# Row skewness of a 1024x8192 matrix: eight input buffers, finer transfers towards the end, and the closing arithmetic split between ScalarE and GpSimd

## The chip, the cores and the metric

The kernel runs on one core of one Trainium2 chip. The core has five engines that this document abbreviates as the profile does: PE (TensorE, matrix multiplies and transposes), DVE (VectorE), ACT (ScalarE), POOL (GpSimd) and SP (SyncE, which here only starts transfers). Sixteen DMA engines move data between the chip's memory and the on-chip buffers. The metric is device time in microseconds of one execution; lower is better.

## The reference

Each of the 1024 rows has 8192 float32 values. For each row the skewness is wanted:

```python
mean = np.mean(x, axis=-1, keepdims=True)
std = np.std(x, axis=-1, keepdims=True)
z = (x - mean) / (std + 1e-8)
return np.mean(z ** 3, axis=-1).astype(np.float32)
```

Both kernels reach it through the three raw moments of a row, m1, m2 and m3 (the means of x, x² and x³): the variance is m2 − m1², and the skewness is (m3 − 3·m1·m2 + 2·m1³) · variance^(−3/2). One pass over the 33.55 MB of input is enough.

## The kernel before

The rows are cut into eight blocks of 128, one row to a partition. A block's 8192 columns are cut into units, and a unit is one transfer, one buffer and one round of work. Block 0 has units of 512, 1024, 2560 and 4096 columns, blocks 1 to 6 have two units of 4096 each, and block 7 has 2048, 2048, 2048, 1024, 512 and 512 (lines 16 and 17): 22 units in all, u0 to u21. One loop runs over them in order.

For a unit, SP starts the transfer into an input buffer x (line 98); there are six such buffers (X_BUFS, line 18), so the transfer of unit u waits until everything that reads unit u−6 has ended. Three engines then work on the unit:

- ACT squares it into a buffer sq, one instruction per unit, and its accumulator gives the unit's share of m2 (line 101).
- DVE multiplies sq by x in one instruction per unit, and its accumulator gives the unit's share of m3 (line 105). It needs the square of the same unit, all of it, so it starts after ACT has ended the unit.
- PE transposes the unit in chunks of 128 columns, all into one PSUM tile tp, where they add up (line 117).

When a block's last unit is through, ACT copies tp to a tile tsb (line 127), PE multiplies tsb by a column of 1/8192, which gives the block's m1 (line 129), and ACT copies that column out of PSUM (line 130). ACT waits for PE between the two copies, for each of the eight blocks, and whatever follows on ACT waits behind.

After the loop, all eight blocks are closed together on tiles of 128x8: two sums over the units' shares (line 136), the products and the variance (lines 150, 151, 167 to 174), a square root on ACT (line 154), a reciprocal with a refining step (lines 156 to 164), the third power (lines 178 and 179) and the last product (line 181). A transpose on PE (line 184), a copy out of PSUM (line 187) and one transfer (line 188) end the program.

Each engine runs its own instructions in program order, and waits for other engines through semaphores that the framework places.

Of the kernel before, what the change touches and what calls it, by code (L numbers as in the profile page):

```python
# [1 line left out]

# [7 lines left out]
FP = mybir.dt.float32  # L10
AF = mybir.ActivationFunctionType
ALU = mybir.AluOpType
X_AXIS = mybir.AxisListType.X

W_MAIN = 4096
FIRST_UNITS = [512, 1024, 2560, 4096]
LAST_UNITS = [2048, 2048, 2048, 1024, 512, 512]
X_BUFS = 6
SQ_BUFS = 5


def _plan_units(NB, C):
    units = []
    for b in range(NB):
        if b == 0:
            ws = FIRST_UNITS
        elif b == NB - 1:
            ws = LAST_UNITS
        else:
            ws = [W_MAIN] * (C // W_MAIN)  # L30
        assert sum(ws) == C
        s = 0
        for w in ws:
            units.append((b, s, s + w))
            s += w
    return units


@with_exitstack
def kernel(  # L40
    ctx: ExitStack,
    tc: tile.TileContext,
    x: bass.AP,
    out: bass.AP,
):
    nc = tc.nc
    P = nc.NUM_PARTITIONS
    R, C = x.shape
    NB = R // P
    inv_n = 1.0 / float(C)  # L50
    import math as _m
    s_scale = float(1.0 / _m.sqrt(C))

    units = _plan_units(NB, C)
    NU = len(units)
    first_unit = {}
    unit_count = {}
    for u, (b, _, _) in enumerate(units):
        first_unit.setdefault(b, u)
        unit_count[b] = unit_count.get(b, 0) + 1  # L60
    MAXC = max(unit_count.values())
    NS = NB * MAXC

    def ucol(u):
        b = units[u][0]
        return b * MAXC + (u - first_unit[b])

    xv = x.rearrange("(b p) c -> b p c", p=P)
    ob = out.rearrange("(b p) -> b p", p=P)

    xpool = ctx.enter_context(tc.tile_pool(name="xp", bufs=X_BUFS))
    sqpool = ctx.enter_context(tc.tile_pool(name="sqp", bufs=SQ_BUFS))
    onep = ctx.enter_context(tc.tile_pool(name="onep", bufs=1))
    psum = ctx.enter_context(tc.tile_pool(name="ps", bufs=2, space=bass.MemoryType.PSUM))
    psum1 = ctx.enter_context(tc.tile_pool(name="ps1", bufs=1, space=bass.MemoryType.PSUM))

    ident = onep.tile([P, P], FP, tag="ident")
    make_identity(nc, ident)
    onesn = onep.tile([P, 1], FP, tag="onesn")
    nc.vector.memset(onesn, inv_n)  # L80

    s2u = onep.tile([P, NS], FP, tag="s2u")
    s3u = onep.tile([P, NS], FP, tag="s3u")
    s1pe = onep.tile([P, NB], FP, tag="s1pe")
    nc.vector.memset(s2u, 0.0)
    nc.vector.memset(s3u, 0.0)

    tiny = onep.tile([P, 8], FP, tag="tiny")
    nc.scalar.activation(out=tiny[:, 0:1], in_=onesn, func=AF.Sqrt)  # L89

    Tsb = [onep.tile([P, P], FP, tag=f"tsb{i}", name=f"tsb{i}") for i in range(2)]

    tp_psum = {}
    for u, (b, cs, ce) in enumerate(units):
        w = ce - cs
        uc = ucol(u)
        xt = xpool.tile([P, w], FP, tag="x", name=f"x_{u}")
        nc.sync.dma_start(out=xt, in_=xv[b, :, cs:ce])  # L98

        sq = sqpool.tile([P, w], FP, tag="sq", name=f"sq_{u}")  # L100
        nc.scalar.activation(  # L101
            out=sq, in_=xt, func=AF.Square, scale=s_scale,
            accum_out=s2u[:, uc : uc + 1],
        )
        nc.vector.scalar_tensor_tensor(  # L105
            out=sq, in0=sq, scalar=1.0, in1=xt, op0=ALU.mult, op1=ALU.mult,
            accum_out=s3u[:, uc : uc + 1],
        )

        if b not in tp_psum:  # L110
            tp_psum[b] = psum.tile([P, P], FP, tag="tp", name=f"tp_{b}")
        tpw = tp_psum[b]
        nchunk = w // P
        firstpe = (u == first_unit[b])
        lastpe = (u == first_unit[b] + unit_count[b] - 1)
        for c in range(nchunk):
            nc.tensor.matmul(  # L117
                out=tpw,
                lhsT=xt[:, c * P : (c + 1) * P],
                rhs=ident,  # L120
                start=(firstpe and c == 0),
                stop=(lastpe and c == nchunk - 1),
                is_transpose=True,
            )
        if lastpe:
            tsb = Tsb[b % 2]
            nc.scalar.copy(out=tsb, in_=tpw)  # L127
            s1ps = psum.tile([P, 1], FP, tag="s1ps", name=f"s1ps_{b}")
            nc.tensor.matmul(out=s1ps, lhsT=tsb, rhs=onesn, start=True, stop=True)  # L129
            nc.scalar.copy(out=s1pe[:, b : b + 1], in_=s1ps)  # L130

    fin = ctx.enter_context(tc.tile_pool(name="fin", bufs=1))

    def blocksum(name, src):
        dst = fin.tile([P, NB], FP, name=name)
        nc.vector.tensor_reduce(  # L136
            out=dst,
            in_=src.rearrange("p (b c) -> p b c", c=MAXC),
            axis=X_AXIS,
            op=ALU.add,  # L140
        )
        return dst

    m1 = s1pe
    m2 = blocksum("s2", s2u)
    m3 = blocksum("s3", s3u)

    m1sq = fin.tile([P, NB], FP)
    var = fin.tile([P, NB], FP)
    nc.vector.tensor_tensor(out=m1sq, in0=m1, in1=m1, op=ALU.mult)  # L150
    nc.vector.tensor_tensor(out=var, in0=m2, in1=m1sq, op=ALU.subtract)  # L151

    sig = fin.tile([P, NB], FP)
    nc.scalar.activation(out=sig, in_=var, func=AF.Sqrt)  # L154
    r0 = fin.tile([P, NB], FP)
    nc.vector.reciprocal(out=r0, in_=sig)  # L156
    t1 = fin.tile([P, NB], FP)
    nc.vector.tensor_tensor(out=t1, in0=r0, in1=r0, op=ALU.mult)  # L158
    nc.vector.tensor_tensor(out=t1, in0=t1, in1=var, op=ALU.mult)  # L159
# [3 lines left out]
    rr = fin.tile([P, NB], FP)  # L163
    nc.vector.tensor_tensor(out=rr, in0=r0, in1=t1, op=ALU.mult)  # L164

    aa = fin.tile([P, NB], FP)
    nc.vector.tensor_tensor(out=aa, in0=m1, in1=m2, op=ALU.mult)
    bb = fin.tile([P, NB], FP)
    nc.vector.tensor_tensor(out=bb, in0=m1sq, in1=m1, op=ALU.mult)
    num = fin.tile([P, NB], FP)  # L170
    nc.vector.scalar_tensor_tensor(
        out=num, in0=aa, scalar=-3.0, in1=m3, op0=ALU.mult, op1=ALU.add
    )
    nc.vector.scalar_tensor_tensor(
        out=num, in0=bb, scalar=2.0, in1=num, op0=ALU.mult, op1=ALU.add
    )
    r3 = fin.tile([P, NB], FP)
    nc.vector.tensor_tensor(out=r3, in0=rr, in1=rr, op=ALU.mult)  # L178
    nc.vector.tensor_tensor(out=r3, in0=r3, in1=rr, op=ALU.mult)  # L179
    skew = fin.tile([P, NB], FP)  # L180
    nc.vector.tensor_tensor(out=skew, in0=num, in1=r3, op=ALU.mult)  # L181

    skT_ps = psum1.tile([NB, P], FP, tag="skT")
    nc.tensor.matmul(out=skT_ps, lhsT=skew, rhs=ident, start=True, stop=True,  # L184
                     is_transpose=True)
    skT = fin.tile([NB, P], FP)
    nc.vector.tensor_copy(out=skT, in_=skT_ps)  # L187
    nc.sync.dma_start(out=ob, in_=skT)

# [29 lines left out]
```

## Time and profile before

| | |
|---|---|
| device time, median of 3 runs | 98.76 us (98.6 to 98.96) |
| span of the profiled execution | 97.4 us |
| median less span | 1.36 us |
| DVE busy | 73.8 us (76%) |
| PE busy | 67.3 us (69%) |
| ACT busy | 65.2 us (67%) |
| POOL busy | 0.7 us (1%), 6 instructions |
| bytes read | 33.55 MB, 344 GB/s over the span |

The span runs from the first to the last instruction of one profiled execution. The records give no device time of that one execution on its own, so the 1.36 us between its span and the median of the runs stand for what lies around it. A time "at 74.88" below is counted in microseconds from the span's start. A timeline row gives the start, the duration, the engine, the line, the operation with its tiles, and in brackets how long the engine had been idle and what released it. A row of the windows view gives a stretch of the span, its length, the busy time of PE, PE's weight loads, DVE, ACT and POOL in it (with the number of instructions), the granted TensorE clock, the busy share of the DMA engines, and the GB/s that they moved.

### The profile page before, as it was taken

To read this page: it belongs to the slowest core of one execution; us is meant where nothing else is said; L and a number is where in the kernel's file an instruction comes from. 1 tells how busy PE (TensorE), PEld (TensorE's weight loads), DVE (VectorE), ACT (ScalarE), POOL (GpSimd) and SP (SyncE) were. 2 spreads that over 40 slices of the span, in tenths; PEclk is the share of its full clock that TensorE was granted. 3 is DMA by queue.
4 is the path that set the end of the run, shared out by engine and by line. 5 is a ranking of instruction groups with operands and counts; after the bars stand their busy time and mean duration, and the time that the engine had idled before them with its cause. 6 is when DMAs were issued, how large, how long until landed. Compare 5 with 4: busy or idle time off the path is not lost.

```text
span 97.4 us, 1323 instructions
## 1 busy us (share of the span) xinstructions
PE 67.3 (69%) x529; PEld 62.2 (64%) x529; DVE 73.8 (76%) x64; ACT 65.2 (67%) x63; POOL 0.7 (1%) x6
## 2 busy tenths in 40 slices
PE   0480969695399999695969596959695998951010
PEld 0260959594398999594959495949594988940000
DVE  0250091498937929999999897989898979999961
ACT  6340909695293899795969597959695998990000
POOL 2000000000000000000000000000000000000000
PEclk9999999999958999999999999999999999999755
DMA  1999999999999999999999999999999993300000
GB/s 61 338 353 446 431 431 431 431 437 431 424 431 431 431 431 417 431 431 424 417 431 431 431 424 431 431 417 431 431 400 417 424 396 146 116 4 0 0 0 2
DMA packets 3190, 33.64 MB, mean 345 GB/s; under 512 B 360, under 2 KB 368, under 8 KB 1008
## 3 DMA queue, kind: packets, MB, share of 16 engines
q1 hardware_dynamic: 3184, 33.56, 82.5%
q8 instruction: 4, 0.07, 0.3%
q14 instruction: 2, 0.02, 0.1%
HBM read 33.55 MB, written 0.00 MB: 344 GB/s over the span
## 4 chain that ended last, share of the span: by engine, by line
DMA 62%; DVE 12%; issue 11%; ACT 7%; PE 4%; SPq 2%; DVEq 0%; ACTq 0%
DMA x<-in_x_dram 62%; DVE sq L105 9%; ACT sq L101 7%; PE tp L117 3%; SPq L98 2%; PE skT_ps L184 0%; DVE skT L187 0%; DVE s L136 0%; DVE t L160 0%; DVE rr L164 0%; DVE skew L181 0%; DVE t L158 0%; DVE r L179 0%; DVE r L178 0%; DVE t L159 0%
## 5 line engine op out<-in xcount | busy, mean ns | idle before, releaser
L105 DVE SCALAR_TENSOR_TENSOR sq<-sq,x 128x4096 f32<-128x4096 f32 (+4 forms) x22 | 71.1, 3260 | 19.9 <-ACT sq L101 19.7
L117 PE MATMUL tp<-ident,x 128*128 128x128 f32 x512 | 64.2, 287 | 17.1 <-DMA x<-in_x_dram 17.1
L117 PEld LDWEIGHTS tp<-ident,x 128*128 128x128 f32 x512 | 60.1, 148 | 19.9 <-DMA x<-in_x_dram 16.5
L101 ACT ACTIVATE sq<-x 128x4096 f32<-128x4096 f32 (+4 forms) x22 | 59.3, 2696 | 16.8 <-DMA x<-in_x_dram 16.8
L129 PEld LDWEIGHTS s1ps<-onesn,tsb 128*128 128x128 f32 x16 | 2.4, 188 | 5.9 <-ACT tsb L127 5.9
L129 PE MATMUL s1ps<-onesn,tsb 128*128 128x1 f32 x16 | 3.1, 260 | 4.0 <-ACT tsb L127 4.0
L184 PE MATMUL skT_ps<-ident,skew 128*8 128x128 f32 x1 | 0.4, 377 | 6.6 <-DVE skew L181 6.6
L184 PEld LDWEIGHTS skT_ps<-ident,skew 128*8 128x8 f32 x1 | 0.1, 84 | 6.7 <-DVE skew L181 6.7
L101 ACT ACTIVATION_READ_ACCUMULATOR sq<-x 128x1 f32 x22 | 4.1, 184 | 0.0
L130 ACT COPY s1pe<-s1ps 128x1 f32<-128x1 f32 x8 | 1.3, 159 | 3.8 <-PE s1ps L129 3.8
L127 ACT COPY tsb<-tp 128x128 f32<-128x128 f32 x8 | 2.1, 260 | 1.8 <-PE tp L117 1.7
L154 ACT ACTIVATE sig<-var 128x8 f32<-128x8 f32 x1 | 0.2, 208 | 4.5 <-DVE var L151 4.5
L105 DVE DVE_READ_ACCUMULATOR sq<-sq,x 128x1 f32 x22 | 1.8, 83 | 0.0
L89 ACT ACT_TABLE_LOAD x1 | 1.3, 1283 | 0.7 <-PEq L203 0.7
L80 DVE MEMSET onesn<- 128x1 f32 x1 | 0.1, 59 | 0.8 <-PEq L203 0.8
L187 DVE COPY skT<-skT_ps 8x128 f32<-8x128 f32 x1 | 0.3, 278 | 0.5 <-PE skT_ps L184 0.5
masks.py:199 POOL TENSOR_SCALAR_AFFINE_SELECT ident<-ident 128x128 f32<-128x128 f32 x1 | 0.3, 292 | 0.1
L89 ACT ACTIVATE tiny<-onesn 128x1 f32<-128x1 f32 x1 | 0.2, 203 | 0.0
masks.py:197 POOL MEMSET ident<- 128x128 f32 x1 | 0.2, 204 | 0.3 <-POOLq L203 0.3
L136 DVE TENSOR_REDUCE s<-s3u 128x8 f32<-128x48 f32 x1 | 0.2, 203 | 0.0
L156 DVE RECIPROCAL r<-sig 128x8 f32<-128x8 f32 x1 | 0.2, 203 | 0.0
L136 DVE TENSOR_REDUCE s<-s2u 128x8 f32<-128x48 f32 x1 | 0.2, 200 | 0.0
(19 smaller groups left out, 2.7 us busy)
## 6 DMA issues: line engine op xcount, KB each, us to landing
x<-in_x_dram SPq DMA_DIRECT2D x13, 2048.0 KB, 21.0
x<-in_x_dram SPq DMA_DIRECT2D x3, 1024.0 KB, 16.2
x<-in_x_dram SPq DMA_DIRECT2D x1, 1280.0 KB, 8.0
x<-in_x_dram SPq DMA_DIRECT2D x2, 512.0 KB, 6.9
x<-in_x_dram SPq DMA_DIRECT2D x3, 256.0 KB, 2.5
out_dram<-skT SPq DMA_DIRECT2D x1, 4.0 KB
```

The costliest lines, as they stand in the source:

```text
L89: nc.scalar.activation(out=tiny[:, 0:1], in_=onesn, func=AF.Sqrt)
L98: nc.sync.dma_start(out=xt, in_=xv[b, :, cs:ce])
L101: nc.scalar.activation(out=sq, in_=xt, func=AF.Square, scale=s_scale, accum_out=s2u[:, uc : uc + 1],)
L105: nc.vector.scalar_tensor_tensor(out=sq, in0=sq, scalar=1.0, in1=xt, op0=ALU.mult, op1=ALU.mult, accum_out=s3u[:, uc : uc + 1],)
L117: nc.tensor.matmul(out=tpw, lhsT=xt[:, c * P : (c + 1) * P], rhs=ident, start=(firstpe and c == 0), stop=(lastpe and c == nchunk - 1), is_ ...
L127: nc.scalar.copy(out=tsb, in_=tpw)
L129: nc.tensor.matmul(out=s1ps, lhsT=tsb, rhs=onesn, start=True, stop=True)
L130: nc.scalar.copy(out=s1pe[:, b : b + 1], in_=s1ps)
L136: nc.vector.tensor_reduce(out=dst, in_=src.rearrange("p (b c) -> p b c", c=MAXC), axis=X_AXIS, op=ALU.add,)
L154: nc.scalar.activation(out=sig, in_=var, func=AF.Sqrt)
L184: nc.tensor.matmul(out=skT_ps, lhsT=skew, rhs=ident, start=True, stop=True, is_transpose=True)
L187: nc.vector.tensor_copy(out=skT, in_=skT_ps)
```

## The change

The change alters five things.

1. **Units.** Blocks 0 to 2 keep their units. The later blocks are cut as in the diff, down to 256 columns for the last unit; there are 31 units instead of 22. There are eight input buffers instead of six.
2. **Slices.** A unit of more than 2304 columns is transferred whole, but ACT and DVE work on it in two slices. There are four sq buffers instead of five, each as large as the largest slice. In the last two units of block 7 ACT writes the square to PSUM, and DVE writes its product to a tile of its own.
3. **Block closing.** All eight m1 columns stay in one PSUM tile. The copy of line 130 is gone, and with it ACT's wait for PE after each block.
4. **Blocks 0 to 6** are closed when block 6 is through, ahead of block 7's work in the program: two sums on DVE, three small ACT instructions that read the m1 columns, and six GpSimd instructions on 128x7, one of them a power with the exponent −1.5.
5. **Block 7** is closed alone on 128x1 tiles: its m2 sum, variance and helpers on ACT, one power on GpSimd, and a sum and two products on DVE. The square root, the reciprocal and the refining step are gone. The rest of the program's end is as before.

```diff
-FIRST_UNITS = [512, 1024, 2560, 4096]
-LAST_UNITS = [2048, 2048, 2048, 1024, 512, 512]
-X_BUFS = 6
-SQ_BUFS = 5
+UNITS = [
+    [512, 1024, 2560, 4096],
+    [4096, 4096],
+    [4096, 4096],
+    [4352, 3840],
+    [3328, 2816, 2048],
+    [2048, 2048, 2048, 2048],
+    [1792, 1792, 1664, 1536, 1408],
+    [1152, 1152, 1152, 1152, 1024, 896, 896, 512, 256],
+]
+SUB_MAX = 2304
+X_BUFS = 8
+SQ_BUFS = 4
+PSUM_SQ = 2
+
+
+def _slices(w):
+    n = -(-w // SUB_MAX)
+    step = -(-w // n // 128) * 128
+    return [(s, min(s + step, w)) for s in range(0, w, step)]
...
+    def finish_first_blocks():
+
+        m2, m3 = small("m2a", L), small("m3a", L)
+        for dst, src in ((m2, s2u), (m3, s3u)):
+            nc.vector.tensor_reduce(
+                out=dst, in_=src.rearrange("p (b c) -> p b c", c=MAXC), axis=X_AXIS, op=ALU.add
             )
...
+        nc.scalar.activation(out=m1sq, in_=s1ps[:, 0:L], func=AF.Square)
+        nc.scalar.activation(out=m1sq3, in_=s1ps[:, 0:L], func=AF.Square, scale=third)
+        nc.scalar.activation(out=nm1, in_=s1ps[:, 0:L], func=AF.Copy, scale=-3.0)
+        g = nc.gpsimd
...
+        g.tensor_tensor(out=var, in0=m2, in1=m1sq, op=ALU.subtract)
+        g.tensor_tensor(out=m1sq3, in0=m1sq3, in1=var, op=ALU.add)
+        g.tensor_tensor(out=m1sq3, in0=m1sq3, in1=nm1, op=ALU.mult)
+        g.tensor_tensor(out=m3, in0=m3, in1=m1sq3, op=ALU.add)
+        g.tensor_tensor(out=rr, in0=var, in1=expo, op=ALU.pow)
+        g.tensor_tensor(out=skew[:, 0:L], in0=m3, in1=rr, op=ALU.mult)
+
+    def close_block(b, tp):
+        tsb = Tsb[b % 2]
+        nc.scalar.copy(out=tsb, in_=tp)
+        nc.tensor.matmul(out=s1ps[:, b : b + 1], lhsT=tsb, rhs=onesn, start=True, stop=True)
...
+            for s, e in _slices(w):
...
+                in_psum = last and k >= len(widths) - PSUM_SQ
+                pool = psq if in_psum else sqpool
+                sq = pool.tile([P, e - s], FP, tag="sq", name=f"sq_{b}_{k}_{s}")
+                nc.scalar.activation(
+                    out=sq, in_=xt[:, s:e], func=AF.Square, scale=s_scale, accum_out=a2
+                )
+                cube = cubes[:, 0 : e - s] if in_psum else sq
+                nc.vector.scalar_tensor_tensor(
+                    out=cube, in0=sq, scalar=1.0, in1=xt[:, s:e],
+                    op0=ALU.mult, op1=ALU.mult, accum_out=a3,
+                )
...
+        close_block(b, tp)
+        if b == L - 1:
+            finish_first_blocks()
...
+    nc.scalar.activation(out=junk, in_=s2l, func=AF.Copy, accum_out=m2)
+    nc.vector.tensor_reduce(out=m3, in_=s3l, axis=X_AXIS, op=ALU.add)
...
+    nc.scalar.activation(out=m1sq, in_=p1, func=AF.Square)
+    nc.scalar.activation(out=var, in_=m1sq, func=AF.Identity, scale=-1.0, bias=m2)
...
+    nc.gpsimd.tensor_tensor(out=rr, in0=var, in1=expo[:, 0:1], op=ALU.pow)
+    nc.scalar.activation(out=nm1, in_=p1, func=AF.Copy, scale=-3.0)
+    nc.scalar.activation(out=v3, in_=m1sq, func=AF.Identity, scale=1.0 / 3.0, bias=var)
     nc.vector.tensor_scalar(
-        out=t1, in0=t1, scalar1=-0.5, scalar2=1.5, op0=ALU.mult, op1=ALU.add
+        out=m3, in0=v3, scalar1=nm1, scalar2=m3, op0=ALU.mult, op1=ALU.add
     )
...
+    nc.vector.tensor_tensor(out=skew[:, L:NB], in0=m3, in1=rr, op=ALU.mult)
```

Here L is 7, the number of the last block, and s1ps is the PSUM tile with the eight m1 columns. The small ACT instruction at the program's start, which draws the activation table in, is a Square instead of a Sqrt.

More of the change, by code (lines that the diff above doesn't have):

```diff
@@ L49 @@
     NB = R // P
+    L = NB - 1
     inv_n = 1.0 / float(C)
[L51 to L66, printed above, removed]
+    s_scale = float(C) ** -0.5
+    third = (1.0 / 3.0) ** 0.5
+    assert len(UNITS) == NB and all(sum(u) == C for u in UNITS)
     xv = x.rearrange("(b p) c -> b p c", p=P)
     ob = out.rearrange("(b p) -> b p", p=P)
+    n_sub = [sum(len(_slices(w)) for w in u) for u in UNITS]
+    MAXC = max(n_sub[:L])
+    NL = n_sub[L]
     xpool = ctx.enter_context(tc.tile_pool(name="xp", bufs=X_BUFS))
@@ L74 @@
     psum = ctx.enter_context(tc.tile_pool(name="ps", bufs=2, space=bass.MemoryType.PSUM))
+    psq = ctx.enter_context(tc.tile_pool(name="psq", bufs=2, space=bass.MemoryType.PSUM))
     psum1 = ctx.enter_context(tc.tile_pool(name="ps1", bufs=1, space=bass.MemoryType.PSUM))
+    onesn = onep.tile([P, 1], FP, tag="onesn")
+    nc.vector.memset(onesn, inv_n)
+    tiny = onep.tile([P, 1], FP, tag="tiny")
+    nc.scalar.activation(out=tiny, in_=onesn, func=AF.Square)
     ident = onep.tile([P, P], FP, tag="ident")
@@ L78 @@
     make_identity(nc, ident)
[L79 to L84, printed above, removed]
+    s2u = onep.tile([P, L * MAXC], FP, tag="s2u")
+    s3u = onep.tile([P, L * MAXC], FP, tag="s3u")
     nc.vector.memset(s2u, 0.0)
     nc.vector.memset(s3u, 0.0)
-    tiny = onep.tile([P, 8], FP, tag="tiny")
-    nc.scalar.activation(out=tiny[:, 0:1], in_=onesn, func=AF.Sqrt)
@@ L91 @@
-    Tsb = [onep.tile([P, P], FP, tag=f"tsb{i}", name=f"tsb{i}") for i in range(2)]
[L93 to L123, printed above, removed]
-            )
[L125 to L150, printed above, removed]
@@ new lines, in close_block @@
+    def close_block(b, tp):
+        tsb = Tsb[b % 2]
+        nc.scalar.copy(out=tsb, in_=tp)
+        nc.tensor.matmul(out=s1ps[:, b : b + 1], lhsT=tsb, rhs=onesn, start=True, stop=True)
+    for b, widths in enumerate(UNITS):
+        last = b == L
+        tp = psum.tile([P, P], FP, tag="tp", name=f"tp_{b}")
+        c0 = 0
+        j = 0
+        for k, w in enumerate(widths):
+            xt = xpool.tile([P, w], FP, tag="x", name=f"x_{b}_{k}")
+            nc.sync.dma_start(out=xt, in_=xv[b, :, c0 : c0 + w])
+            c0 += w
+            for s, e in _slices(w):
+                i = b * MAXC + j
+                a2 = s2l[:, j : j + 1] if last else s2u[:, i : i + 1]
+                a3 = s3l[:, j : j + 1] if last else s3u[:, i : i + 1]
+                j += 1
+                in_psum = last and k >= len(widths) - PSUM_SQ
[9 more added lines that the diff above has]
+                )
+            n = w // P
+            for c in range(n):
+                nc.tensor.matmul(
+                    out=tp, lhsT=xt[:, c * P : (c + 1) * P], rhs=ident,
+                    start=(k == 0 and c == 0), stop=(c0 == C and c == n - 1),
+                    is_transpose=True,
+                )
+        close_block(b, tp)
+        if b == L - 1:
+            finish_first_blocks()
@@ L168 @@
[L168 to L179, printed above, removed]
@@ L180 @@
-    skew = fin.tile([P, NB], FP)
-    nc.vector.tensor_tensor(out=skew, in0=num, in1=r3, op=ALU.mult)
+    nc.vector.tensor_tensor(out=skew[:, L:NB], in0=m3, in1=rr, op=ALU.mult)
     skT_ps = psum1.tile([NB, P], FP, tag="skT")
-    nc.tensor.matmul(out=skT_ps, lhsT=skew, rhs=ident, start=True, stop=True,
-                     is_transpose=True)
-    skT = fin.tile([NB, P], FP)
+    nc.tensor.matmul(out=skT_ps, lhsT=skew, rhs=ident, start=True, stop=True, is_transpose=True)
+    skT = small("skT", P)[0:NB, :]
```

44 lines of the change are left out of this document (16 added, 28 removed).

## The prediction

> **What bounds the kernel now.** I read the page's slices first, then the chain, then the timeline of the end.
>
> ```profile
> DVE  0250091498937929999999897989898979999961
> DMA  1999999999999999999999999999999993300000
> GB/s 61 338 353 446 431 431 431 431 437 431 424 431 431 431 431 417 431 431 424 417 431 431 431 424 431 431 417 431 431 400 417 424 396 146 116 4 0 0 0 2
> DMA 62%; DVE 12%; issue 11%; ACT 7%; PE 4%; SPq 2%; DVEq 0%; ACTq 0%
> ```
>
> The transfers run at 431 GB/s up to about 80 us, then thin out, and from about 85 us on nothing arrives. The last twelve microseconds belong to DVE and to the closing arithmetic. So there are two stages: a stream, which the DMA engines set, and an end, which is the place to save. The timeline shows the end:
>
> ```profile
> 55.30 3.66 ACT L101 ACTIVATE sq<-x 128x4096 f32<-128x4096 f32 x1 [1.18 <-DMA x<-in_x_dram]
> 65.09 3.64 ACT L101 ACTIVATE sq<-x 128x4096 f32<-128x4096 f32 x1 [1.17 <-DMA x<-in_x_dram]
> 74.88 3.66 ACT L101 ACTIVATE sq<-x 128x4096 f32<-128x4096 f32 x1 [1.18 <-DMA x<-in_x_dram]
> 78.66 4.43 DVE L105 SCALAR_TENSOR_TENSOR sq<-sq,x 128x4096 f32<-128x4096 f32 x1 [0.50 <-ACT sq L101]
> 83.01 2.29 DVE L105 SCALAR_TENSOR_TENSOR sq<-sq,x 128x2048 f32<-128x2048 f32 x1
> 85.22 2.29 DVE L105 SCALAR_TENSOR_TENSOR sq<-sq,x 128x2048 f32<-128x2048 f32 x1
> 89.65 1.22 DVE L105 SCALAR_TENSOR_TENSOR sq<-sq,x 128x1024 f32<-128x1024 f32 x1
> 90.80 0.69 DVE L105 SCALAR_TENSOR_TENSOR sq<-sq,x 128x512 f32<-128x512 f32 x1
> 91.41 0.69 DVE L105 SCALAR_TENSOR_TENSOR sq<-sq,x 128x512 f32<-128x512 f32 x1
> 92.02 0.20 DVE L136 TENSOR_REDUCE s<-s2u 128x8 f32<-128x48 f32 x1
> 92.14 0.20 DVE L136 TENSOR_REDUCE s<-s3u 128x8 f32<-128x48 f32 x1
> ```
>
> Each ACT row was released by a landing, so these are landing times. The three rows are two units apart: 9.79 us for 8192 columns (4.19 MB), or 428 GB/s. Block 6's last unit, u15, lands at 74.88, ACT holds it to 78.6, and DVE takes it only from 78.66 to 83.01. Only then does DVE begin block 7, and it works without a gap until 92.02: 9.01 us for 8192 columns in six pieces. ACT has squared all of block 7 by then. The price of large units is thus the time from 74.88 to 83.01, in which a whole unit passes first through ACT and then through DVE.
>
> DVE's price by size, from one start to the next: 0.61 us for 512 columns (90.80 to 91.41), 1.15 for 1024, 2.21 for 2048, 4.35 for 4096. That is 1.045 ns a column and some 0.075 us a piece. A 4096 unit lands every 4.89 us, so DVE can keep up with the stream, and it can't catch up by much.
>
> **The transfers.**
>
> ```profile
> SPq L98 <- DVE sq L105: 73.8, 16, 7.4
> 78.23 5.26 SPq L98 DMA_DIRECT2D x<-in_x_dram  x2
> 4.90:7.00 2.10, 1.94 (x8) 1.54 (x8) 0.97 (x1) 1.10 (x2) 0.00 (x0) 1.00 0.96 341
> 78.00:79.00 1.00, 1.00 (x12) 1.00 (x10) 0.50 (x3) 1.00 (x3) 0.00 (x0) 1.00 1.02 414
> 80.00:81.00 1.00, 0.58 (x6) 0.34 (x5) 1.00 (x1) 0.67 (x3) 0.00 (x0) 1.00 0.79 305
> 81.00:82.00 1.00, 1.00 (x11) 1.00 (x12) 1.00 (x1) 0.86 (x2) 0.00 (x0) 1.00 0.40 150
> 82.00:83.00 1.00, 1.00 (x12) 1.00 (x11) 1.00 (x1) 1.00 (x1) 0.00 (x0) 1.00 0.12 47
> 83.00:84.00 1.00, 1.00 (x12) 1.00 (x10) 1.00 (x3) 1.00 (x3) 0.00 (x0) 1.00 0.04 16
> ```
>
> SP waits for DVE nearly always, but up to 79 us the engines stay full, so the wait costs nothing there, and two more buffers gain nothing in the stream. They matter at the end: u20 was started at 78.23 and u21 only about 83.2, when DVE had freed u15. With eight buffers the last transfer waits for block 7's first unit, which DVE leaves at about 80, some 5 us ahead of its turn. The windows from 80 to 84 also show that the sixteen engines don't end together: their mean share after 80 adds up to 0.79 + 0.40 + 0.12 + 0.04 = 1.35 us, yet two of them still work at 82 to 83 and one until about 83.6.
>
> More transfers cost something. At 78 to 79, with 1 MB units and full engines, 414 GB/s stand against 428: 1.05 MB takes 2.53 instead of 2.45 us, about 0.08 a transfer. Bounds: nothing, and 0.13 (half a megabyte at 305/0.79 = 386 GB/s against 428). I take 0.07. Up to the end of block 6 there are 22 transfers instead of 16, so its last unit lands at 74.88 + 6 x 0.07 = 75.3 (75.0 to 75.7), and all has landed at 75.3 + 9.79 + 7 x 0.07 = 85.6, counting nine transfers against two.
>
> The Trainium skill, "DMA: Bandwidth & Descriptors", section "Rules for kernel authors", speaks against this part: it asks for at least 1 MiB per transfer, and its measured table has 341 GB/s for one of 1 MB. Here 1 MB transfers run at 414 GB/s among others that are queued, so the trace disagrees for that size. By the page's rate the landings would be the bound, and the sum some 98.7 us (an estimate; rival C works out the same from a row of the trace).
>
> **From block 6 to block 7.** Units of 1792 down to 1408 columns land, by 1.195 ns a column, more slowly than DVE's 1.045 takes them, so no backlog has built up.
>
> ```profile
> 3.35 0.63 ACT L101 ACTIVATE sq<-x 128x512 f32<-128x512 f32 x1 [1.12 <-DMA x<-in_x_dram]
> 4.10 0.69 DVE L105 SCALAR_TENSOR_TENSOR sq<-sq,x 128x512 f32<-128x512 f32 x1 [3.10 <-ACT sq L101]
> DVE sq L105 <- ACT sq L101: 19.7, 13, 4.8
> 80.43 0.24 ACT L127 COPY tsb<-tp 128x128 f32<-128x128 f32 x1
> 80.96 5.44 PE L117 MATMUL tp<-ident,x 128*128 128x128 f32 x48
> 81.14 0.16 ACT L130 COPY s1pe<-s1ps 128x1 f32<-128x1 f32 x1 [0.47 <-PE s1ps L129]
> 81.21 1.92 ACT L101 ACTIVATE sq<-x 128x2048 f32<-128x2048 f32 x1
> 83.12 1.92 ACT L101 ACTIVATE sq<-x 128x2048 f32<-128x2048 f32 x1
> 85.02 1.05 ACT L101 ACTIVATE sq<-x 128x1024 f32<-128x1024 f32 x1
> 86.06 0.62 ACT L101 ACTIVATE sq<-x 128x512 f32<-128x512 f32 x1
> ```
>
> ACT takes 1.91 us for 2048 columns and 1.04 for 1024, 0.85 ns a column. The 1408 columns that land at 75.3 are squared at 75.3 + 1.37 = 76.67; PE's 11 transposes (0.113 each) are through by 76.6. The copy of tp starts at 76.67, and the m1 column can be read 0.71 us later (80.43 to 81.14), at 77.38. The seven waits like this one that block closing had are gone but for this one and the last; they lay beside the stream and gain nothing. Here, though, three reads (0.07 each, 81.14 to 81.21) stand before block 7's first square, so it starts at 77.6, not at its landing, 76.8. What is queued behind this wait on ACT are block 7's squares, and DVE waits for them.
>
> From a square's start to DVE's start are 0.75 us at 512 columns (3.35 to 4.10), so 0.75 + 640 x 0.00085 = 1.29 at 1152: DVE begins block 7 at **78.9**. It ended block 6 at 75.3 + 1.37 + 0.14 + 1.55 = 78.4 and has done its two sums (0.12 apart) by then.
>
> Block 7 is nine pieces instead of six, 9.01 + 3 x 0.075 = 9.24 us, so DVE ends at **88.14** if it never waits. It doesn't: its last piece, 256 columns (0.34 us), lands at 85.6, and ACT has squared it by 86.3. DVE bounds the end by about a microsecond over the transfers. Writing the last two squares to PSUM, and DVE reading them there, shows in no row; I bound it by 0.1 us either way for two small pieces, and take nothing. The finer slices elsewhere cost DVE some 16 x 0.075 = 1.2 us inside the stream, where it waits for ACT anyway (19.7 us in total); without that cover they would count in full.
>
> **The closing.**
>
> ```profile
> 94.34 0.17 DVE L181 TENSOR_TENSOR skew<-num,r 128x8 f32<-128x8 f32 x1
> 95.28 0.37 SPq L188 DMA_DIRECT2D out_dram<-skT  x1
> masks.py:199 POOL TENSOR_SCALAR_AFFINE_SELECT ident<-ident 128x128 f32<-128x128 f32 x1 | 0.3, 292 | 0.1
> L203 POOL MEMSET const-float32-0.0<- 128x1 f32 x1 | 0.1, 98 | 0.2 <-issue 0.2
> L89 ACT ACT_TABLE_LOAD x1 | 1.3, 1283 | 0.7 <-PEq L203 0.7
> ```
>
> Before, from DVE's last piece (92.02) to the last product (94.34) are 2.32 us. After, DVE has the m3 sum at 88.14 + 0.12, a dependent product 0.22 later and the last product 0.20 after that (dependent steps of before are 0.2 apart): it starts at **88.68**. That is 5.66 us ahead of 94.34. From there to the end nothing changes (97.4 − 94.34 = 3.06).
>
> ACT's and POOL's part must be ready by then. After the last landing at 85.6 come ACT's last square (to 86.2), the copy of tp, and m1 0.71 later (86.9); the m2 sum lies in that wait. Two dependent ACT steps at about 0.21 give the variance at 87.35, and the other two end by 87.8. The power on POOL starts at 87.35. No row shows a power or a two-input POOL instruction: the nearest are 0.10 us (128x1 memset) and 0.29 (128x128 select), and a far end is the longest fixed cost of any row, 1.28. I take 0.29, as its data are as small. It is then ready at 87.7, and up to 1.3 us it stays hidden behind DVE. The six POOL instructions for blocks 0 to 6 lie beside 9 us of DVE work, and whether they disturb it is the second rival.
>
> **Sum.** 97.4 − 5.66 = 91.74 us of span, and 1.36 us around it: **93.1 us** against the median of 98.76. Of the 5.66, 83.01 − 78.9 = 4.1 come from DVE's earlier start on block 7, less 0.23 for three more pieces, and 2.32 − 0.54 = 1.78 from the shorter closing.
>
> **The rivals.**
>
> *A, the small transfers land slower than 414 GB/s, mildly.* At 386 GB/s for blocks 6 and 7 (from 65.09, 8.39 MB in 21.7 us) all has landed at 86.8. Then the closing follows the landing: the power ends at 86.8 + 1.75 + 0.29 = 88.85, the last product starts then, and the time is 93.3; with a power of 1.28 us it is 94.3. For it: the row of 80 to 81. Against: that row is half empty already.
>
> *B, POOL and DVE hold each other up.* Six POOL instructions fall into DVE's bound stretch. If each makes DVE wait for its own length, 6 x 0.29 = 1.7 us are added (94.8); by the far end for the two powers, and waiting for a gap at the end, 2.7 to 3 (96). If they only wait for DVE, nothing is added before the last power. No row has POOL at work beside line 105, so the trace is silent, and with six instructions in nine pieces I give B the largest chance after the forecast. The Trainium skill, "GPSIMD Engine Reference", section "Key points", says that the two share their SBUF interfaces and contend where a DVE instruction has two SBUF inputs, as line 105 has; no run here shows it yet.
>
> *C, slower than before.* If transfers of 1 MB and less land at 341 GB/s, as the window of 4.9 to 7.0 had it with half a megabyte and more under way, blocks 5 to 7 (12.58 MB from 55.30) land only at 92.2. With 2.04 to the last product, 3.06 and 1.36 it is 98.7. The point of no gain is a landing at 92.3, 12.58 MB in 37.0 us: below 340 GB/s over these blocks the kernel is slower, and by the next step down, 330, it is 99.9. Against: 414 GB/s at 78 to 79, with the same sizes in the middle of the queue. The window of 341 is the start, with the queue still filling.
>
> *D, better than the sum.* The slowest DMA engine sets a landing, and the others are some 2.3 us ahead of it on average (81.35 against 83.6). If smaller units spread this lag, block 7 starts up to 1.5 us sooner: 91.6.
>
> *E, nothing gained:* 98.5 to 99. The change would have to leave DVE's start on block 7 at 83, for instance because a buffer isn't freed before the whole of a large unit is through. Block 6 has no large unit, so this is unlikely.
>
> **How the numbers follow.** Forecast (92.3 to 94.0): 0.53. A above that: 0.12. B: 0.17. D: 0.10. C: 0.05. E: 0.03. The range takes in B but for its far end, and most of D: **91.7 to 95.6**. A measurement of this kernel tells about 0.3% from no change, so faster 0.92, same 0.03, slower 0.05.
>
> **What would show it.** Right: the engines stay full past 80 us and the last landing is near 85.6; DVE starts block 7 near 79 and has no gap to 88; from its last piece to the last product it is 0.55 us. Wrong: gaps on DVE released by ACT in block 7 (then the landings bound it, A or C); pieces of line 105 longer than 1.28 us at 1152 columns, or gaps released by POOL (B); the last product waiting for POOL (a power beyond 1.3 us); a second table load on ACT, which would cost 1.28 us wherever it stands.

## The result and the profile after

| | before | after |
|---|---|---|
| device time, median | 98.68 us (97.52 to 98.96, 4 runs) | 92.35 us (92.12 to 93.16, 4 runs) |
| ratio, 95% interval | | 0.9385 (0.931 to 0.9459) |
| span of the profiled execution | 97.4 us | 91.4 us (its own time was 93.16) |
| DVE busy | 73.8 us (76%) | 73.9 us (81%) |
| ACT busy | 65.2 us | 69.1 us |
| POOL busy | 0.7 us, 6 instructions | 9.4 us, 14 instructions |

The kernel is 6.2% faster; the forecast was 93.1 us. The profiled execution of after is the slowest of its four runs (the others have spans of 90.3 to 90.8), which matters below. The slices of its page:

```profile
POOL 3000000000000000000000000000000000699820
DMA  1999999999999999999999999999999999991000
GB/s 43 362 374 440 445 438 409 430 452 430 402 423 452 442 417 434 435 424 399 430 414 404 430 420 420 423 407 422 419 409 423 406 418 408 406 344 74 0 0 2
```

A slice is now 2.29 us. The hole that the transfers had from 80 to 85 us is gone: they run full until about 81 us and then thin out. The windows of after (same columns as before) show it finer:

```profile
79.00:80.00 1.00, 0.94 (x9) 0.87 (x9) 1.00 (x3) 0.95 (x3) 0.92 (x2) 1.00 1.02 404
81.00:82.00 1.00, 0.90 (x8) 0.67 (x7) 1.00 (x1) 0.96 (x3) 1.00 (x1) 1.00 0.84 309
82.00:83.00 1.00, 1.00 (x9) 0.79 (x9) 1.00 (x3) 1.00 (x3) 1.00 (x1) 1.00 0.43 162
83.00:84.00 1.00, 0.91 (x7) 0.67 (x8) 1.00 (x3) 1.00 (x3) 1.00 (x2) 1.00 0.13 48
84.00:85.00 1.00, 1.00 (x9) 1.00 (x10) 1.00 (x3) 0.97 (x4) 0.92 (x2) 1.00 0.03 10
```

With transfers of 576 KB on the way, the engines still move 404 GB/s at full share. The last of them works until about 84.5 (0.03 of 16 engines is half a microsecond of one), so everything has landed near 84.5. The timeline of the end:

```profile
74.88 1.38 ACT L135 ACTIVATE sq<-x 128x1408 f32<-128x1408 f32 x1 [0.16 <-DMA x<-in_x_dram]
76.50 1.62 DVE L139 SCALAR_TENSOR_TENSOR sq<-sq,x 128x1408 f32<-128x1408 f32 x1
76.51 1.17 ACT L135 ACTIVATE sq<-x 128x1152 f32<-128x1152 f32 x1
77.67 0.17 ACT L101 ACTIVATE m1sqa<-s1ps 128x7 f32<-128x7 f32 x1
78.04 0.19 DVE L97 TENSOR_REDUCE m2a<-s2u 128x7 f32<-128x42 f32 x1
78.28 1.34 DVE L139 SCALAR_TENSOR_TENSOR sq<-sq,x 128x1152 f32<-128x1152 f32 x1
79.55 1.35 DVE L139 SCALAR_TENSOR_TENSOR sq<-sq,x 128x1152 f32<-128x1152 f32 x1
86.56 0.68 DVE L139 SCALAR_TENSOR_TENSOR cubes<-sq,x 128x512 f32<-128x512 f32 x1
87.29 0.56 POOL L163 TENSOR_TENSOR rrl<-varl,expo 128x1 f32<-128x1 f32 x1 [0.60 <-ACT varl L161]
87.34 0.42 DVE L139 SCALAR_TENSOR_TENSOR cubes<-sq,x 128x256 f32<-128x256 f32 x1
87.81 0.16 DVE L157 TENSOR_REDUCE m3l<-s3l 128x1 f32<-128x9 f32 x1
88.09 0.28 DVE L166 TENSOR_SCALAR m3l<-v3l,nm1l,m3l 128x1 f32<-128x1 f32 x1
88.47 0.16 DVE L169 TENSOR_TENSOR skew<-m3l,rrl 128x1 f32<-128x1 f32 x1
```

DVE begins block 7 at 78.28 instead of 83.01, ends it at 87.69 (0.12 before the sum at 87.81) instead of 92.02, and has the last product at 88.47 instead of 94.34. These are gains of 4.73 at block 7's start, less 0.40 in the block, and 1.54 in the closing; together 5.87 of the 6.0 us between the two spans.

Where DVE's idle time went is the more telling view. These three rows are the last in the timeline of DVE, up to the end of block 7, that show an idle time:

```profile
41.39 2.43 DVE L139 SCALAR_TENSOR_TENSOR sq<-sq,x 128x2176 f32<-128x2176 f32 x1 [0.79 <-ACT sq L135]
64.39 2.29 DVE L139 SCALAR_TENSOR_TENSOR sq<-sq,x 128x2048 f32<-128x2048 f32 x1 [0.71 <-ACT sq L135]
66.90 2.29 DVE L139 SCALAR_TENSOR_TENSOR sq<-sq,x 128x2048 f32<-128x2048 f32 x1 [0.20 <-ACT sq L135]
41.40:87.70 46.30, 38.23 (x312) 33.58 (x310) 45.30 (x56) 41.02 (x66) 8.48 (x7) 1.00 0.90 367
```

The fourth row is a window: DVE works 45.30 of 46.30 us. Before, a gap of 0.44 to 0.50 us stood in front of every 4096 unit from 54 to 79 us, as in these rows:

```profile
54.16 4.42 DVE L105 SCALAR_TENSOR_TENSOR sq<-sq,x 128x4096 f32<-128x4096 f32 x1 [0.45 <-ACT sq L101]
73.73 4.43 DVE L105 SCALAR_TENSOR_TENSOR sq<-sq,x 128x4096 f32<-128x4096 f32 x1 [0.45 <-ACT sq L101]
```

From 41 us on DVE now sets the pace, and the landings do so only where one is late (at 62.35, which DVE's waits at 64.39 and 66.90 follow). By the end of block 6, though, DVE has nearly caught up: it starts the last piece, of 1408 columns, at 76.50, 0.24 us after ACT has ended its square (74.88 + 1.38).

### The profile page after: what moved, and what is told of

The parts are those of the page before. It is cut to its first block, busy times and chain, and to the rows that moved or that the text cites. A ratio compares the mean times of both kernels' runs of the same rounds, so it can differ in the third digit from the quotient of the medians.

```text
span 91.4 us, 1437 instructions
## 1 busy us (share of the span) xinstructions
PE 68.0 (74%) x529; PEld 60.6 (66%) x529; DVE 73.9 (81%) x91; ACT 69.1 (76%) x101; POOL 9.4 (10%) x14
## 5 line engine op out<-in xcount | busy, mean ns | idle before, releaser
L139 DVE SCALAR_TENSOR_TENSOR sq<-sq,x 128x2048 f32<-128x2048 f32 (+11 forms) x39 | 71.5, 1885 | 13.9 <-ACT sq L135 13.9
L145 PE MATMUL tp<-ident,x 128*128 128x128 f32 x512 | 65.2, 285 | 15.3 <-DMA x<-in_x_dram 15.0
L135 ACT ACTIVATE sq<-x 128x2048 f32<-128x2048 f32 (+12 forms) x41 | 62.8, 1534 | 17.4 <-DMA x<-in_x_dram 15.9
L145 PEld LDWEIGHTS tp<-ident,x 128*128 128x128 f32 x512 | 58.7, 147 | 20.5 <-DMA x<-in_x_dram 16.6
L106 POOL TENSOR_TENSOR vara<-m2a,m1sqa 128x7 f32<-128x7 f32 x1 | 1.3, 1294 | 77.1 <-DVE m3a L97 77.1
L135 ACT ACTIVATION_READ_ACCUMULATOR sq<-x 128x1 f32 x41 | 7.6, 186 | 0.0
L139 DVE DVE_READ_ACCUMULATOR sq<-sq,x 128x1 f32 x39 | 3.2, 83 | 0.0
L110 POOL TENSOR_TENSOR rra<-vara,expo 128x7 f32<-128x7 f32 x1 | 2.6, 2624 | 0.0
L107 POOL TENSOR_TENSOR m1sq3a<-m1sq3a,vara 128x7 f32<-128x7 f32 x1 | 1.2, 1202 | 0.1
L139 DVE SCALAR_TENSOR_TENSOR cubes<-sq,x 128x512 f32<-128x512 f32 (+1 forms) x2 | 1.1, 554 | 0.1
L108 POOL TENSOR_TENSOR m1sq3a<-m1sq3a,nm1a 128x7 f32<-128x7 f32 x1 | 1.1, 1150 | 0.0
```

The costliest lines, as they stand in the source:

```text
L106: g.tensor_tensor(out=var, in0=m2, in1=m1sq, op=ALU.subtract)
L107: g.tensor_tensor(out=m1sq3, in0=m1sq3, in1=var, op=ALU.add)
L108: g.tensor_tensor(out=m1sq3, in0=m1sq3, in1=nm1, op=ALU.mult)
L110: g.tensor_tensor(out=rr, in0=var, in1=expo, op=ALU.pow)
L135: nc.scalar.activation(out=sq, in_=xt[:, s:e], func=AF.Square, scale=s_scale, accum_out=a2)
L139: nc.vector.scalar_tensor_tensor(out=cube, in0=sq, scalar=1.0, in1=xt[:, s:e], op0=ALU.mult, op1=ALU.mult, accum_out=a3,)
```

## The experiments

Each kernel ran on a chip beside the kernel before. Times are medians with their range; the ratio is to the kernel before on the same chip. A time without a range is that of a single run.

### The changed kernel again

> The changed kernel once more, unaltered. The profiled execution of it had a late landing at 62.35 us (3.56 us after the one before, where 2.45 is usual); DVE then waited 0.71 us and had no gap after 66.90. Theory: that landing is chance, and without it DVE has gaps up to block 7; median 92.1 to 92.6, and a span near 90.3 to 90.8. Rival: the late landing belongs to the kernel; it comes again, with a span of 91.4.

Measured: 93.27 us (92.83 to 93.6), ratio 0.9512 (0.9461 to 0.9562). A third set, on another chip, gave 93.40 (92.69 to 93.95), ratio 0.9484 (0.941 to 0.9558):

> The changed kernel unaltered, to stand beside the next two on the same chip: 92.3 to 93.3 us.

Neither half of the first expectation held as put. The late landing didn't come at 62, but both profiles have one elsewhere, at 25.62 and at 25.91, with spans of 91.5 and 91.8. So late landings are usual and their place is not fixed. The forecast of 93.1 lies among these medians; the first set was the fastest of the three.

### The closing alone, and the units alone

```diff
 # closing_only: the changed kernel with
-UNITS = [
...
+UNITS = [[512, 1024, 2560, 4096]] + [[4096, 4096]] * 6 + [[2048, 2048, 2048, 1024, 512, 512]]
-SUB_MAX = 2304
+SUB_MAX = 4096
-X_BUFS = 8
-SQ_BUFS = 4
-PSUM_SQ = 2
+X_BUFS = 6
+SQ_BUFS = 5
+PSUM_SQ = 0
```

> Only the closing is changed: units, six input buffers and whole-unit squares are those of before; blocks 0 to 6 are closed ahead of block 7 on GpSimd, block 7 on ACT, GpSimd and DVE as after. Theory: from DVE's last piece to the last product it takes 0.78 us instead of 2.32, the two sums for blocks 0 to 6 put 0.24 in front of block 7, and the end is 0.13 shorter: 98.7 - 1.4 = 97.3 us. DVE still starts block 7 near 83. Rival (the six GpSimd instructions and the power hold DVE up): pieces of line 105's kind get longer or wait, 98 or more.

```diff
 # units_only: the kernel before with the units, X_BUFS = 8 and SQ_BUFS = 4 of the changed one, and
...
+        for s, e in _slices(w):
+            uc = ucol(u)
+            sq = sqpool.tile([P, e - s], FP, tag="sq", name=f"sq_{u}_{s}")
...
+                out=sq, in_=xt[:, s:e], func=AF.Square, scale=s_scale,
...
+                out=sq, in0=sq, scalar=1.0, in1=xt[:, s:e], op0=ALU.mult, op1=ALU.mult,
```

> Only the units, the slices and the buffers are changed (eight input, four square); the closing and the copy of m1 after each block are those of before. Theory: DVE starts block 7 near 78.3 instead of 83.0 and needs some 0.3 more for three pieces more: 98.7 - 4.4 = 94.3 us. With closing_only the two savings should add up to that of the whole change, about 6 us. Rival (the gain is mostly the closing's): above 96.

Measured: closing_only 97.58 us (96.41 to 98.62), ratio 0.9883 (0.9821 to 0.9945); units_only 94.72 (94.14 to 95.75), ratio 0.965 (0.9591 to 0.9708). By the theories it was 97.3 and 94.3. The savings are 1.2% and 3.5%, 4.7% together, where the whole change gave 4.9% on the same chip. They add up, and the units, with their slices and buffers, bring three quarters.

In closing_only one thing was not as expected. These are rows of its timeline:

```profile
81.48 2.28 DVE L130 SCALAR_TENSOR_TENSOR sq<-sq,x 128x2048 f32<-128x2048 f32 x1
81.71 2.11 POOL L97 TENSOR_TENSOR vara<-m2a,m1sqa 128x7 f32<-128x7 f32 x1 [80.41 <-ACT sq L126]
90.94 0.56 POOL L154 TENSOR_TENSOR rrl<-varl,expo 128x1 f32<-128x1 f32 x1
91.53 0.16 DVE L160 TENSOR_TENSOR skew<-m3l,rrl 128x1 f32<-128x1 f32 x1 [0.31 <-POOL rrl L154]
```

A subtraction on 128x7 takes POOL 2.11 us and ends at 83.82, just after the DVE piece that began at 81.48 (83.76). Beside DVE's large pieces POOL is so late that the last product waits for its power. In the changed kernel, with smaller pieces, it doesn't.

### Six input buffers

```diff
-X_BUFS = 8
+X_BUFS = 6
```

> The changed kernel with six input buffers instead of eight. Theory: the buffers matter at the very end alone; the last transfer waits for the unit six before it, which DVE left at 83.4, so it lands near 86 and DVE gets its last 256 columns at most 0.3 us late: 92.3 to 92.8 us. Rival (eight buffers keep the stream full while units get small): the DMA share drops below 0.95 in blocks 5 to 7 and the kernel is 1 to 3 us slower, 93.5 to 95.5.

Measured: 94.05 us (92.11 to 94.75), ratio 0.9583 (0.9503 to 0.9662), against 0.9512 (0.9461 to 0.9562) for eight on the same chip. The intervals overlap; a cost of up to some 1.6 us (the difference of the ratios with their intervals) is neither shown nor excluded. In its profile, of the fastest of its runs, the DMA share stays at 1.00 to 1.02 from 39 to 80 us, no landing is late after the first units, DVE has no gap released by ACT after 41.31, and the span is 90.3 us, that of the changed kernel's fastest runs. So with punctual landings six buffers do as well as eight. That eight pay when one is late would fit the wider spread, but was not tried by itself.

### Without slices

```diff
-SUB_MAX = 2304
+SUB_MAX = 4352
-SQ_BUFS = 4
+SQ_BUFS = 3
```

> The changed kernel without slices: ACT and DVE take each unit whole (31 pieces instead of 41), with three square buffers. Theory (DVE has no gap from 41 us on, so its end is set by when it starts that stretch): it gets the 4352 unit, which lands near 39.3, after 3.9 us of ACT instead of 2.1, and later saves some 4 x 0.075 us for pieces that are gone: 1.4 to 1.6 us slower than the changed kernel, 94.5 to 95 us. Rival (the prediction's picture, in which DVE is current with the landings up to block 6 and only the sizes of blocks 6 and 7 count): no slower, or 0.1 to 0.3 faster.

Measured: 94.87 us (94.69 to 95.2), ratio 0.9619 (0.9571 to 0.9667). That is 1.5 us more than the changed kernel's 93.40, measured on another chip, and 1.1 to 1.3 us more by the ratios, although DVE has ten pieces less. The theory holds: what slices save is the time from the landing of a large unit to DVE's start, and DVE doesn't get it back by block 7. Its timeline:

```profile
44.60 4.69 DVE L139 SCALAR_TENSOR_TENSOR sq<-sq,x 128x4352 f32<-128x4352 f32 x1 [0.74 <-ACT sq L135]
75.04 1.38 ACT L135 ACTIVATE sq<-x 128x1408 f32<-128x1408 f32 x1 [0.16 <-DMA x<-in_x_dram]
78.30 1.62 DVE L139 SCALAR_TENSOR_TENSOR sq<-sq,x 128x1408 f32<-128x1408 f32 x1
79.95 1.35 DVE L139 SCALAR_TENSOR_TENSOR sq<-sq,x 128x1152 f32<-128x1152 f32 x1
```

The first row is DVE's last wait before the end; block 7 then starts at 79.95. The 4352 unit lands at 40.63 here (a landing at 25.79 was late) and DVE has it 3.97 us later. With slices this is 2.15 us, from 39.24 to 41.39. At the end of block 6 DVE is still 1.88 us behind (from 75.04 + 1.38 to 78.30), where with slices it is 0.24 behind. The three square buffers are no rival: DVE has no idle time from 44.60 to the end of block 7 but for some 0.1 us in front of the last piece, so it waits for no square, and ACT's waits from 35 to 75 us are for landings.

### What GpSimd's instructions cost

First, four of the six instructions for blocks 0 to 6 on DVE (all but the power and the last product):

```diff
-        g.tensor_tensor(out=var, in0=m2, in1=m1sq, op=ALU.subtract)
+        nc.vector.tensor_tensor(out=var, in0=m2, in1=m1sq, op=ALU.subtract)
...
```

> The changed kernel, but four of the six GpSimd instructions for blocks 0 to 6 (all but the power and the last product) run on DVE. Theory (DVE works without a gap from about 41 us on, and GpSimd costs it nothing): four dependent small steps of 0.1 to 0.2 us stand in front of block 7 on DVE and are paid in full, +0.4 to +0.8 us against the changed kernel, 93.2 to 94 us where that runs at 92.3 to 93.3. Rival B (GpSimd holds DVE up): same or faster.

Measured: 93.69 us (93.13 to 94.35), ratio 0.9579 (0.9512 to 0.9646). It isn't faster, as B would have it, and by the ratios not clearly slower either. The trace shows a price: a 1152 piece and the next are 1.65 us apart around two of the moved instructions, where 1.28 is usual. From the two sums to the last product it is 11.02 us (77.86 to 88.88), against 10.43 in the changed kernel (78.04 to 88.47), so all four cost about 0.6 us, as the theory has it:

```profile
78.24 1.35 DVE L139 SCALAR_TENSOR_TENSOR sq<-sq,x 128x1152 f32<-128x1152 f32 x1
79.52 0.16 DVE L107 TENSOR_TENSOR m1sq3a<-m1sq3a,vara 128x7 f32<-128x7 f32 x1
79.78 0.17 DVE L108 TENSOR_TENSOR m1sq3a<-m1sq3a,nm1a 128x7 f32<-128x7 f32 x1
79.89 1.36 DVE L139 SCALAR_TENSOR_TENSOR sq<-sq,x 128x1152 f32<-128x1152 f32 x1
```

Second, the same kinds of instruction where DVE is idle:

```diff
...
+    for op in (ALU.subtract, ALU.add, ALU.mult, ALU.add):
+        nc.gpsimd.tensor_tensor(out=tb, in0=ta, in1=expo, op=op)
+    nc.gpsimd.tensor_tensor(out=tb, in0=ta, in1=expo, op=ALU.pow)
+    nc.gpsimd.tensor_tensor(out=tb, in0=ta, in1=tb, op=ALU.mult)
```

> The changed kernel with six more GpSimd instructions of the same kinds and size (128x7, on constants, used by nothing) at the program's start, where DVE is idle until its first piece at about 4.3 us and has gaps up to 16 us. Theory: the two engines share a way to the buffers and GpSimd is the one that waits; with DVE idle the plain instructions take 0.2 to 0.5 us, where they took 0.93 to 1.29 beside DVE, and the power less than 2.6. Rival: the length is GpSimd's own; they take 0.9 to 1.3 here too.

The kernel took 93.39 us in a single run. The first block of rows is POOL's timeline there, at the start (the first row joins the four plain ones). The second is POOL's timeline in the changed kernel, in block 7:

```profile
1.31 1.04 POOL L89 TENSOR_TENSOR tb<-ta,expo 128x7 f32<-128x7 f32 x4
2.42 1.51 POOL L90 TENSOR_TENSOR tb<-ta,expo 128x7 f32<-128x7 f32 x1
4.01 0.20 POOL L91 TENSOR_TENSOR tb<-ta,tb 128x7 f32<-128x7 f32 x1
```

```profile
78.39 1.29 POOL L106 TENSOR_TENSOR vara<-m2a,m1sqa 128x7 f32<-128x7 f32 x1 [77.08 <-DVE m3a L97]
79.76 1.20 POOL L107 TENSOR_TENSOR m1sq3a<-m1sq3a,vara 128x7 f32<-128x7 f32 x1
80.92 2.62 POOL L110 TENSOR_TENSOR rra<-vara,expo 128x7 f32<-128x7 f32 x1
83.52 1.15 POOL L108 TENSOR_TENSOR m1sq3a<-m1sq3a,nm1a 128x7 f32<-128x7 f32 x1
```

Alone, a plain one takes 0.26 us (1.04 for four) and the power 1.51. Beside DVE they take 1.15 to 1.29 and 2.62. They end at 79.68, 80.96, 83.54 and 84.67; the DVE pieces beside them end at 79.62, 80.90, 83.46 and 84.61. Each POOL instruction ends 0.06 to 0.08 after a DVE piece does: it waits for the piece to end. The theory holds here.

Third, heavy GpSimd work on 128x512:

```diff
...
+    for _ in range(24):
+        nc.gpsimd.tensor_tensor(out=tb, in0=ta, in1=ta, op=ALU.add)
```

> The changed kernel with 24 more GpSimd additions of 128x512 (constants, used by nothing) from the program's start. This asks whether GpSimd work lengthens DVE's pieces. Theory: it doesn't; a DVE piece of 128x2048 stays at 2.29 us and 128x1280 at 1.49 where GpSimd is busy beside it, and the time stays within 0.5 us. Rival B: the pieces beside GpSimd work take longer, or wait in between, by some tenths of a microsecond each.

Measured: 100.78 us in a single run, and here the theory falls. In this kernel's timeline DVE's pieces grow:

```profile
16.17 2.30 DVE L144 SCALAR_TENSOR_TENSOR sq<-sq,x 128x2048 f32<-128x2048 f32 x1 [1.86 <-ACT sq L140]
18.40 3.12 DVE L144 SCALAR_TENSOR_TENSOR sq<-sq,x 128x2048 f32<-128x2048 f32 x1
21.45 3.12 DVE L144 SCALAR_TENSOR_TENSOR sq<-sq,x 128x2048 f32<-128x2048 f32 x1
```

A piece that follows another at once takes 3.12 us instead of 2.29; the one at 16.17, after a pause, takes 2.30. The two engines take turns: between two DVE pieces one POOL instruction goes through, and DVE waits for it, 0.83 us per 128x512 addition (the shortest addition in the trace takes 1.04 us). Rival B's mechanism is real. With 128x7 the price is too small to see: the 1152 pieces average 1350 ns in the changed kernel, with POOL beside them, and 1350 ns in units_only, where POOL does nothing. The gaps between the pieces don't grow either. These are rows of units_only:

```profile
79.32 1.35 DVE L118 SCALAR_TENSOR_TENSOR sq<-sq,x 128x1152 f32<-128x1152 f32 x1
87.61 0.68 DVE L118 SCALAR_TENSOR_TENSOR sq<-sq,x 128x512 f32<-128x512 f32 x1
```

From block 7's first piece to its piece of 512 columns it is 8.29 us there and 8.28 in the changed kernel (78.28 to 86.56), with GpSimd's instructions beside it.

### Where the late landings come from

```diff
-            n = w // P
+            n = max(1, w // P // 4)
```

> The changed kernel with a quarter of the transposes: only a quarter of each unit's columns goes into m1, so PE has some 780 instructions less. This asks where the late landings come from (26.08 in the profile of before, 62.35 in that of after, none in two others). In all of them the instruction queue q8 fetches four 16 KB packets, each about 1.05 us of one DMA engine's time. Theory: these fetches are PE's program, and a late landing is a fetch on the engine that is already the slowest; with a quarter of the instructions there are no or one q8 packets after 15 us, no landing is late, and all runs lie near the lower end, 91.8 to 92.3 us. Rival (late landings come from memory or from PE's clock): the runs spread by 1 us or more as before.

This kernel leaves out three quarters of what m1 is made of, so it serves for the timing alone. Measured: 93.05 us (92.41 to 93.65), ratio 0.9499 (0.9426 to 0.9572). The first row is from the view of the transfers of the kernel before, in the stretch from 20 to 25 us, right ahead of the late landing at 26.08. The second is this kernel's, from 15 to 90 us, where that of after shows four. The columns are packets, MB, and the time that they took as a share of 16 engines:

```profile
q8 instruction: 1, 0.02, 1.3%
```

```profile
q8 instruction: 1, 0.02, 0.1%
```

In the first, 1.3% of 16 engines for 5 us is 1.04 us of one engine for one packet. Three of four packets went with PE's instructions, so these fetches are mostly PE's program: that part holds. The spread didn't go: it is 1.2 us here, although the granted clock was 1.0 in all six runs, so PE's clock isn't what spreads them. In this profile no landing is late after 15 us, but the third unit landed at 10.25 instead of 9.36, and the span is again 91.4. So the fetches aren't the whole cause, and they don't always cost something: six_buffers has four of them after 15 us and no late landing. That a fetch delays a landing when it falls on the engine that is behind fits the traces, but isn't shown.

### Two attempts at a faster version

```diff
 # units_2048: blocks 0 to 5 in units of 2048 after the first three, SUB_MAX = 2560, and
-X_BUFS = 8
+X_BUFS = 13
```

> The changed kernel with units of 2048 from block 0's end to block 5 (block 0: 512, 1024, 2560, 2048, 2048; 38 transfers instead of 31, 40 pieces as against 41) and thirteen input buffers of at most 2560 columns; blocks 6 and 7 as they are. Theory: since DVE has no gap from 41 us on, its end is set by how far behind the landings it is there; a 4096 unit puts it 4.89 us of landing behind, a 2048 unit half of that, so DVE gets up to 2 us ahead and the landings (7 x 0.07 = 0.5 us later) become the bound, 0.5 to 1 us sooner than now: 91.4 to 92.4, against the changed kernel of the same call. Rival (the landings bound block 7 already): 7 transfers more cost 0.5 us, 92.8 to 93.8.

```diff
 # seven_pieces
-    [1152, 1152, 1152, 1152, 1024, 896, 896, 512, 256],
+    [1536, 1408, 1280, 1152, 1024, 896, 896],
...
-PSUM_SQ = 2
+PSUM_SQ = 0
```

> The changed kernel with block 7 in seven units (1536, 1408, 1280, 1152, 1024, 896, 896) instead of nine, the squares all in SBUF. Theory (DVE bounds block 7 and the last landing has a microsecond to spare): two pieces less save 2 x 0.075 and the gap of 0.1 us at the PSUM pieces, -0.1 to -0.3 us. Rival (the last landing bounds the end, which is why the transfers shrink to 256): the last unit passes ACT and DVE in 1.1 + 0.95 instead of 0.5 + 0.35 us, and the kernel is 0.5 to 1.2 us slower.

Measured beside 93.40 for the changed kernel: units_2048 93.71 us (92.53 to 94.1), ratio 0.9485 (0.9399 to 0.957); seven_pieces 93.69 (93.5 to 94.15), ratio 0.9524 (0.9463 to 0.9584). Neither can be told from the changed kernel, so neither theory's gain is there, and neither rival's loss.

With units_2048, DVE waits about 0.18 us for each 2048 unit up to 67 us and then starts block 7 at 78.62, as the changed kernel did at 78.69 in the third set: it stayed closer to the landings early and had less left to catch up. The changed kernel had caught up by then as well, so a smaller lag in the middle gains nothing more. With seven_pieces, DVE's two saved pieces went into a wait:

```profile
78.85 1.76 DVE L139 SCALAR_TENSOR_TENSOR sq<-sq,x 128x1536 f32<-128x1536 f32 x1 [0.40 <-ACT sq L135]
```

A larger first unit of block 7 keeps ACT 0.33 us longer, and DVE, done with block 6, waits 0.40 for it. No version beat the changed kernel.

## Why the prediction was right

**The size.** 93.1 was forecast; three sets gave 92.35, 93.27 and 93.40. That the profiled execution took 93.16 us is luck in part, for the errors below cancel. In the span they are −0.62 us at DVE's start on block 7, +0.17 in the block, +0.24 in the closing and −0.13 behind it, −0.34 together (91.4 instead of 91.74); what lies around the span was 0.40 more than forecast.

**The landings.** Block 6's last unit was put at 75.3 and landed at 74.88; the last at 85.6 and came near 84.5. That block 6's last landing is at 74.88 both before and after doesn't show that six more transfers cost nothing: each profile holds a late landing, of 1.76 us before and 1.11 after. Two profiles without one compare better, closing_only with the units of before and six_buffers with those of after:

```profile
73.28 3.63 ACT L126 ACTIVATE sq<-x 128x4096 f32<-128x4096 f32 x1 [1.18 <-DMA x<-in_x_dram]
73.72 1.38 ACT L135 ACTIVATE sq<-x 128x1408 f32<-128x1408 f32 x1 [0.15 <-DMA x<-in_x_dram]
```

That is 0.44 us for six transfers, 0.07 each, as forecast. A, C and E fell with the windows: 404 GB/s at 576 KB, and DVE's start on block 7 at 78.28. D's 91.6 wasn't reached by any run, and its lag is still there in the profile: the shares after 81 add up to 0.84 + 0.43 + 0.13 + 0.03 = 1.43, so the engines end at 82.4 on average, 2.1 us ahead of the last.

**The buffers.** Two more were to matter at the end, by starting the last transfer sooner. With punctual landings they don't: six_buffers has the changed kernel's shortest span, 90.3 us, in its fastest run.

**DVE's start on block 7.** 78.9 was forecast, 78.28 measured, but not by the chain that was worked out. The three reads of m1 were put in front of block 7's first square. The rows have the square at 76.51 and the reads at 77.67: they run behind it, so ACT did not wait. DVE waited for nobody either; it came straight from block 6 and the two sums.

**The slices.** The step "no backlog has built up" named no condition, and the slices were priced at nothing because DVE "waits for ACT anyway". This was the weak step. DVE has no such cover from 41 us on, and without the slices a backlog does build up: 1.88 us at the end of block 6 in no_slices, which is 1.5 us slower, against 0.24 in the changed kernel. The number came out right because the changed kernel has the slices; the account would have given the same start without them, and been wrong. That much was luck.

**Block 7.** 9.24 us were forecast for nine pieces, 9.41 measured. The 0.17 stand in front of the last piece, which starts 0.78 us after the piece of 512 columns, where 0.61 is usual. These are the two pieces with their squares in PSUM, which were priced at nothing; what in them costs the time isn't shown.

**The closing.** 0.54 us was forecast from the last piece to the last product, 0.78 measured. The two dependent steps were mis-sized: 0.28 and 0.38 instead of 0.22 and 0.20. The first of them takes 0.28 us itself, with two per-row operands, where the same operation with two constants took 0.17 before (line 160, 128x8). The rest after it took 2.93 instead of 3.06.

**GpSimd.** Plain instructions were taken at 0.29 us and took 0.93 to 1.29. That was mis-sized and free: it is waiting for DVE. The last power was taken at 0.29 and took 0.56; it was ready at 87.85, 0.62 before its use. So it stayed hidden, as forecast, and B's cost did not come at this size (8.28 us for the first seven pieces, 8.29 without GpSimd). The Trainium skill, "GPSIMD Engine Reference", section "Key points", names contention where a DVE instruction has two SBUF inputs. The trace agrees: POOL's 0.26 us became 1.15 to 1.29, and with 128x512 DVE paid 0.83 us a piece.

**What lies around the span.** The 1.36 us was too small. In the runs that list both, time and span are 1.7 to 1.9 us apart, so the profiled execution of before was one of about 99.2 us, above the median. The landing at 26.08, 6.65 us after the one before instead of 4.89, fits this; closing_only's profile, which has no late landing, is of the shortest of its runs, 96.41 us of 96.41 to 98.62. The forecast should have read it as one late landing and not as the kernel's pace. After has such landings too, so most of the error fell out of the difference, which the forecast had not foreseen.

## What to carry to other kernels

When a chain of two engines follows a stream that the second can barely keep up with, the second engine's lag at the largest unit can decide the end, not only the last units: look for its last idle time, count everything after it, and see whether it has caught up by the last units. Where it has, less lag gains nothing. Cut what the first engine hands over more finely than what is transferred; it costs a few hundredths of a microsecond a piece and saves half of the first engine's time on the unit. In these runs tiny GpSimd steps (128x7) beside a busy DVE were free to DVE but slow, so give them time; large ones (128x512) were paid by both.

## What the runs showed of the hardware

- GpSimd and DVE took turns: a 128x7 GpSimd instruction of 0.26 us took 2.11 us beside a DVE piece of 2.28 us, and a 128x512 addition lengthened each DVE piece that followed another from 2.29 to 3.12 us.
- A power on GpSimd took 1.51 us for 128x7 alone and 0.56 for 128x1 at the program's end.
- The same program's landings shifted by about a microsecond from run to run: the third unit landed between 9.2 and 10.3 us, and one of the later landings often came 0.9 to 1.8 us late (1.76 before, 1.11, 1.46 and 1.33 in three profiles of after, 0.9 in pool_at_start). An instruction fetch of 16 KB took 1.04 us of one DMA engine.
- Queued transfers of 576 KB kept 404 GB/s (after, 79 to 80 us), where those of 2 MB had 431 (before).
